# 384 bytes more in front of the left tiles of SBUF

## The chip, the cores and the metric

The kernel runs on one core of a Trainium2 chip. The metric is the device time of one execution in microseconds; the median of the runs counts. Names used below: PE is TensorE with its matmuls, PEld its weight loads, DVE is VectorE, ACT ScalarE, POOL GpSimd, SP SyncE (which issues most DMAs).

## What is computed

One layer of a decoder on 512 tokens of width 1024, in float32:

```python
h = h + 0.5 * swiglu(rmsnorm(h, ffn1_norm), ffn1_w_gate, ffn1_w_up, ffn1_w_down)   # 1024 -> 2816 -> 1024
proj = rmsnorm(h, mix_norm) @ w_in
u, v, z, xbc, dt_raw = split(proj)
ya = rmsnorm(chunked_spatial_gating(gelu(u), gelu(v), ...), gm_out_norm)
yb = mamba2_mixer(z, xbc, dt_raw, ...)
h = h + concatenate([ya, yb]) @ w_out
h = h + 0.5 * swiglu(rmsnorm(h, ffn2_norm), ffn2_w_gate, ffn2_w_up, ffn2_w_down)
h = h + sigmoid(rmsnorm(h, ple_norm) @ ple_w_gate + ple_b_gate) * (p @ ple_w_proj)
return rmsnorm(h, final_norm)
```

## The kernel before

The activations lie feature by feature: a tile is 128 features by 512 tokens, `h` is eight of them. Every large product is made of three matmuls in a rounded format (fp32r): an operand is split into a high part (`hi`, a copy rounded to fp32r) and a low part (`lo`, the rest), and `passes` (L468) issues hi by hi, hi by lo and lo by hi into one PSUM bank. For each unit of weights a DMA brings `raw` (128 by 1024), ACT makes `whi` from it and DVE `wlo` (`Unit.split` L438, `Parts.split` L682). A matmul has a stationary operand, 128 by 128 elements that a weight load brings into the array, and a moving operand that is streamed past it. In the profile's names `b<-x,whi` the moving operand stands first: `x` streams past `whi`.

The stages, in order of time:

- FFN 1 and FFN 2 (`swiglu`, L1028): the gate and up products of the groups 1 to 10 are done with seven products instead of eight for a 2-by-2 split (`Group.steps`, L869). The moving operands are the sums and differences of the input's halves, 256 tokens wide, in tiles `xfa` and `xfb` (`XForms`, L704); the stationary ones are `whi` and `wlo`. The products of group 0 (`plain_steps`, L930) take the same tiles with 512 tokens, in two runs of 256. The down products take `ghi` and `glo` as moving operands and `whix`, `wlox` (or `whi`, `wlo`) as weights.
- The mixer: `projection` (L1199), `first_step` and `dt_step` take the sixteen tiles `x` as moving operands, 512 wide, and `whi`, `wlo` as weights. `v_step` (L1544) turns this round: `whi` and `wlo` move, 512 wide, and 128-column slices of `x` are the weights. Then `out_step` (L1762) takes `ya` and `yb` as moving operands, with `whi`, `wlo`.
- The last stage (L1833 and on, here called PLE): eight units, `x` moving, 512 wide for the first five and in halves of 256 for the last three.

All operations are recorded and then issued in a fixed order, a list of some 2,500 units (`ORDER`, L87), by `issue` (L1935, the instruction itself at L1943, which is why every row of the profile says L1943).

SBUF of a partition is laid out so. A base pool `sb` holds what lives all the time: constants, `tmp`, `h`, `raw`, `whi`, `wlo` and small tiles. Above it stands a left region, and from the top end a right region is filled downwards. Each is opened anew as the stages go (`open_region` L336, `open_now` L342): left for FFN 1, for the mixer, for FFN 2 and for PLE, right for FFN 1, the mixer, FFN 2 and PLE. A new region's tiles may lie where tiles of the old one lay, and then wait for just those tiles (`reuse_waits="tile"`). Ahead of the tiles of a left region `open_now` puts a tile that nobody uses, `pad` (L331), of as many bytes per partition as `PAD` (L61) says:

```python
    def pad(pool, name):
        n = PAD[name.replace("1", "").replace("2", "")]
        if n:
            pool.tile([P, n // 4], F32, tag="pad", name=name_of("pad"))
```

From the order and the sizes of the tiles follows where each set begins in a partition. The base pool ends at byte 90,976. With the `PAD` of before:

| tiles | region | first byte | bytes each | remainder by 512 |
|---|---|---|---|---|
| `whi`, `wlo` (3 each) | base | 54,144 and 66,432 | 4,096 | 384 |
| `h`, `tmp`, `raw` | base | 25,472, 19,328, 41,856 | 2,048, 2,048, 4,096 | 384 |
| `xfa` (2), `xfb` (2) | left, FFN | 91,072 and 107,456 | 8,192 and 20,480 | 448 |
| `x` (16) | left, mixer and PLE | 91,136 | 2,048 | 0 |
| `xs` (8), `u` (9); `emb` (8) | left, mixer; PLE | 123,904 and 140,288; 123,904 | 2,048 | 0 |
| `ghi`, `glo`, `whix`, `wlox` | right, FFN | from 159,712 on | 4,096 | 480 |
| `ya`, `yb` (16 each) | right, mixer | 163,712 and 196,480 | 2,048 | 384 |

Within a tile, each weight load begins at a multiple of 512 bytes, and the moving operand of each fp32r matmul at a multiple of 1,024 (of 512 where `whi` and `wlo` move), so the remainder holds for all operands of a set. Copies of `raw0`, `F` and `embt` stand at the end of the FFN's left region.

Of the kernel before, what the change touches and what calls it, by code (L numbers as in the profile page):

```python
# [57 lines left out]

PAD = {"sb": 0, "ffn_left": 96, "mix_left": 160, "ple_left": 160, "ffn_right": 0, "mix_right": 96, "ple_right": 0}  # L61
HEADS = 16
HD = 64
GROUPS = 2
# [218 lines left out]
def layer_kernel(ctx: ExitStack, tc: tile.TileContext, a: dict, out: bass.AP):  # L283
# [47 lines left out]
# [4 lines that stand above are left out]
# [1717 lines left out]
```

## Time and profile before

| | us |
|---|---|
| three runs | 1115.97, 1113.59, 1114.28 |
| median of the runs | 1114.28 |
| the profiled execution | 1115.11 |
| its span, first to last instruction | 1113.4 |
| mean granted TensorE clock in it | 0.993 |

A row of instructions has the line, the engine and the operation, out<-in by the names of the tiles, the shape, the count, and then the busy time in us and the mean ns of one. The recorded duration of a matmul is longer than the distance from its start to the next one's start, since matmuls overlap in the array. What a matmul costs in a stream is that distance, and it is read from the timeline: the start of one row, the start of a later one, and the number of matmuls between. In a row of the timeline the first column is the start, the second the length of the merged row, and x2 says that it holds two matmuls. In a row of windows stand the stretch, its length, then the busy time and the count of each engine, the granted clock, the share of the DMA engines and GB/s.

### The profile page before, as it was taken

How to read it: one execution, taken by the hardware profiler on the slowest of the kernel's cores; microseconds unless marked ns; L12 is line 12 of the kernel's file. 1: busy time of each engine (PE TensorE's matmuls, PEld its weight loads, DVE VectorE, ACT ScalarE, POOL GpSimd, SP SyncE). 2: the span in 40 equal slices, each digit the busy share in tenths (PEclk: the TensorE clock that was granted, in tenths of full speed). 3: DMA queues.
4: the chain of work that ended last, by engine and by line, in shares of the span. 5: the costliest groups of instructions: out<-in, count | busy, mean ns of one | idle time of the engine just before them, and what ended most of it. 6: DMA issues, size and time to landing. Idle time of an engine off the chain costs nothing.

```text
span 1113.4 us, 16384 instructions
## 1 busy us (share of the span) xinstructions
PE 1099.0 (99%) x6631; PEld 967.6 (87%) x6631; DVE 765.0 (69%) x1072; ACT 520.2 (47%) x715; POOL 127.5 (11%) x124
## 2 busy tenths in 40 slices
PE   8999999999999999999999999999999999999996
PEld 6899999999998777778877878899999999999886
DVE  6977666666667468766649876687765666766656
ACT  7544443434435336866424444455434433434445
POOL 1100010000000200123103000101100000000212
PEclk9999999999999999999999999999999999999997
DMA  9788468564631224542314133767837674643412
GB/s 318 207 213 245 109 202 229 146 190 133 152 95 57 82 90 153 160 136 79 114 62 133 38 106 122 208 184 179 217 93 204 169 204 139 166 103 123 133 38 76
DMA packets 49036, 161.66 MB, mean 145 GB/s; under 512 B 5568, under 2 KB 5824, under 8 KB 48960
## 3 DMA queue, kind: packets, MB, share of 16 engines
q1 hardware_dynamic: 34128, 117.46, 31.3%
q0 software_dynamic: 9232, 33.56, 16.3%
q10 hardware_dynamic: 5600, 9.60, 2.9%
q8 instruction: 52, 0.85, 0.3%
q14 instruction: 24, 0.20, 0.1%
HBM read 156.33 MB, written 4.26 MB: 144 GB/s over the span
## 4 chain that ended last, share of the span: by engine, by line
PE 92%; DVE 5%; DMA 1%; ACT 1%; issue 1%; POOL 0%; ACTq 0%; SPq 0%; POOLq 0%
PE b L1943 92%; DVE tmp L1943 1%; DVE wlo L1943 1%; DVE xs L1943 1%; DMA g<-in_p 1%; DVE u L1943 0%; DVE x L1943 0%; DVE h L1943 0%; POOL ssum L1943 0%; DVE ya L1943 0%; DMA cs_dram<-csrow 0%; DVE yb L1943 0%; ACT tmp L1943 0%; DVE convin L1943 0%; ACT whi L1943 0%
## 5 line engine op out<-in xcount | busy, mean ns | idle before, releaser
L1943 PE MATMUL b<-xfb,whi 128*128 128x256 f32 (+1 forms) x1664 | 305.8, 284 | 0.0
L1943 PEld LDWEIGHTS b<-xfb,whi 128*128 128x128 f32 x1664 | 259.2, 188 | 7.0 <-issue 1.0
L1943 PE MATMUL b<-xfb,wlo 128*128 128x256 f32 (+1 forms) x832 | 236.3, 284 | 0.0
L1943 DVE TENSOR_TENSOR wlo<-raw,whi 128x1024 fp32r<-128x1024 f32 (+1 forms) x139 | 173.8, 1254 | 66.3 <-ACT whi L1943 66.3
L1943 ACT CAST whi<-raw 128x1024 fp32r<-128x1024 f32 (+1 forms) x140 | 145.1, 1040 | 147.5 <-PE b L1943 107.4
L1943 PE MATMUL b<-x,whi 128*128 128x512 f32 (+1 forms) x640 | 189.3, 382 | 0.7 <-ACT x L1943 0.4
L1943 PEld LDWEIGHTS b<-xfb,wlo 128*128 128x128 f32 x832 | 156.2, 188 | 1.4
L1943 PEld LDWEIGHTS b<-x,whi 128*128 128x128 f32 x640 | 116.1, 188 | 26.5 <-issue 1.5
L1943 PE MATMUL b<-xfa,whi 128*128 128x256 f32 (+1 forms) x704 | 134.4, 289 | 0.0
L1943 PE MATMUL b<-x,wlo 128*128 128x512 f32 (+1 forms) x312 | 117.9, 378 | 0.3 <-DVE wlo L1943 0.3
L1943 PE MATMUL b<-ghi,whix 128*128 128x512 f32 x296 | 116.6, 394 | 0.0
L1943 PE MATMUL b<-ghi,wlox 128*128 128x512 f32 x296 | 116.5, 394 | 0.0
L1943 PE MATMUL b<-glo,whix 128*128 128x512 f32 x296 | 115.3, 390 | 0.0
L1943 PEld LDWEIGHTS b<-xfa,whi 128*128 128x128 f32 x704 | 110.8, 188 | 3.9
L1943 PE MATMUL b<-xfa,wlo 128*128 128x256 f32 (+1 forms) x352 | 102.0, 290 | 0.0
L1943 ACT CAST whi<-rawb 128x1024 fp32r<-128x1024 f32 x52 | 54.5, 1048 | 79.7 <-PE b L1943 56.0
L1943 DVE TENSOR_TENSOR wlo<-rawb,whi 128x1024 fp32r<-128x1024 f32 x52 | 63.3, 1221 | 40.8 <-ACT whi L1943 40.7
L1943 DVE SCALAR_TENSOR_TENSOR h<-b,h 128x512 f32<-128x512 f32 x96 | 64.3, 685 | 29.3 <-PE b L1943 28.9
L1943 ACT CAST whix<-rawd 128x1024 fp32r<-128x1024 f32 (+1 forms) x40 | 39.4, 986 | 84.1 <-PE b L1943 73.2
L1943 PEld LDWEIGHTS b<-x,wlo 128*128 128x128 f32 x312 | 58.7, 188 | 12.6 <-DVE wlo L1943 1.0
L1943 PEld LDWEIGHTS b<-xfa,wlo 128*128 128x128 f32 x352 | 66.1, 188 | 1.4
L1943 DVE TENSOR_TENSOR wlox<-rawd,whix 128x1024 fp32r<-128x1024 f32 (+1 forms) x40 | 45.6, 1140 | 31.1 <-ACT whix L1943 31.1
(229 smaller groups left out, 1644.0 us busy)
## 6 DMA issues: line engine op xcount, KB each, us to landing
raw<-in_ffn_gu SPq DMA_DIRECT2D x56, 512.0 KB, 5.6
rawd<-in_ffn_down SPq DMA_DIRECT2D x40, 512.0 KB, 4.5
rawb<-in_ffn_gu SPq DMA_DIRECT2D x32, 512.0 KB, 5.7
raw<-in_ffn_gu POOLq DMA_DIRECT2D x30, 512.0 KB, 7.6
raw<-in_w_in SPq DMA_DIRECT2D x29, 512.0 KB, 3.7
s<-in_ffn_gu SPq DMA_DIRECT2D x20, 512.0 KB, 5.5
s<-in_ffn_gu POOLq DMA_DIRECT2D x20, 512.0 KB, 7.7
raw<-in_w_out SPq DMA_DIRECT2D x16, 512.0 KB, 3.7
```

The lines of the kernel that those rows point to most:

```text
L1943: getattr(getattr(real, engine), what)(*(real_of(x) for x in args), **{k: real_of(x) for k, x in kw.items()})
```

## The change

The three left layouts get 384 bytes more of the unused tile in front. Nothing else is changed: the same instructions in the same order.

```diff
-PAD = {"sb": 0, "ffn_left": 96, "mix_left": 160, "ple_left": 160, "ffn_right": 0, "mix_right": 96, "ple_right": 0}
+PAD = {"sb": 0, "ffn_left": 480, "mix_left": 544, "ple_left": 544, "ffn_right": 0, "mix_right": 96, "ple_right": 0}
```

So `xfa` and `xfb` begin at 91,456 and 107,840 (remainder by 512: 320 in place of 448), `x` at 91,520 (384 in place of 0), `xs`, `u` and `emb` at remainder 384 in place of 0. The base pool and the right regions stay.

## The prediction

> **What bounds the kernel.** I read the busy times and the chain of waits on the page first, then the groups of PE instructions by form, then windows, then the timeline of PE.
>
> ```profile
> span 1113.4 us, 16384 instructions
> PE 1099.0 (99%) x6631; PEld 967.6 (87%) x6631; DVE 765.0 (69%) x1072; ACT 520.2 (47%) x715; POOL 127.5 (11%) x124
> PE 92%; DVE 5%; DMA 1%; ACT 1%; issue 1%; POOL 0%; ACTq 0%; SPq 0%; POOLq 0%
> ```
>
> PE is busy 99% of the span and carries 92% of the chain that ends last. So the time is, nearly, the sum of the distances between matmul starts, and a change that touches these distances reaches the end almost undiminished.
>
> ```profile
> L1943 PE MATMUL b<-xfb,whi 128*128 128x256 f32 x1600 | 285.9, 279 | 0.0
> L1943 PE MATMUL b<-xfb,wlo 128*128 128x256 f32 x800 | 223.8, 280 | 0.0
> L1943 PE MATMUL b<-x,whi 128*128 128x512 f32 x544 | 172.1, 399 | 0.7 <-ACT x L1943 0.4 <-DVE x L1943 0.3
> L1943 PE MATMUL b<-xfa,whi 128*128 128x256 f32 x640 | 114.5, 279 | 0.0
> L1943 PE MATMUL b<-x,wlo 128*128 128x512 f32 x264 | 104.4, 395 | 0.3 <-DVE wlo L1943 0.3
> L1943 PE MATMUL b<-xfa,wlo 128*128 128x256 f32 x320 | 89.5, 280 | 0.0
> L1943 PE MATMUL b<-whi,x 128*128 128x512 f32 x128 | 42.7, 401 | 0.0
> L1943 PE MATMUL b<-wlo,x 128*128 128x512 f32 x64 | 25.3, 396 | 0.7 <-DVE wlo L1943 0.7
> ```
>
> These are the matmuls that read a tile on the left side. With `x`, 512 wide: 544 + 264 + 128 + 64 = 1000. With `xfa`, `xfb`, 256 wide: 1600 + 800 + 640 + 320 = 3360. What one costs in a stream stands in the timeline of PE. Here are, in pairs, the first and the last row of undisturbed stretches; in all of them one row is a lo and the next holds two hi, so a step from one lo row to the next is three matmuls.
>
> ```profile
> 672.64 0.39 PE L1943 MATMUL b<-ya,wlo 128*128 128x512 f32 x1
> ...
> 691.00 0.39 PE L1943 MATMUL b<-ya,wlo 128*128 128x512 f32 x1
> ```
>
> ```profile
> 400.72 0.39 PE L1943 MATMUL b<-x,wlo 128*128 128x512 f32 x1
> ...
> 414.72 0.39 PE L1943 MATMUL b<-x,wlo 128*128 128x512 f32 x1
> 421.76 0.39 PE L1943 MATMUL b<-x,wlo 128*128 128x512 f32 x1
> ...
> 424.55 0.39 PE L1943 MATMUL b<-x,wlo 128*128 128x512 f32 x1
> ```
>
> The first pair spans 81 matmuls in 18.36 us: 226.7 ns each (`ya`, on the right side). The second spans 60 in 14.00: 233.3 ns; the third 12 in 2.79: 232.5. Same form, same weights `whi` and `wlo`, yet `x` is 6.2 ns dearer on average of its two paces (232.9). The clock is not the reason:
>
> ```profile
> 367.00:427.00 60.00, 59.86 (x266) 48.09 (x267) 34.70 (x74) 21.37 (x28) 5.98 (x4) 1.00 0.26 81
> 427.00:452.00 25.00, 24.03 (x114) 18.98 (x113) 21.91 (x36) 16.70 (x26) 2.39 (x2) 1.00 0.56 173
> 655.00:712.00 57.00, 57.00 (x250) 46.68 (x251) 38.09 (x52) 26.79 (x38) 0.00 (x0) 1.00 0.43 138
> ```
>
> It is 1.00 in the windows of `x` (first row) and of `ya` (last). What differs is where the tiles lie. By the table of the layout, `ya` and the weights have the same remainder by 512 (384); `x` has 0, a distance of 128. I read the rows so: while one matmul streams, the next one's weights are read, and the two reads of SBUF disturb each other by an amount that depends on their distance modulo 512. That is an inference from the pace at two distances.
>
> Now the 256-wide stream:
>
> ```profile
> 760.48 0.28 PE L1943 MATMUL b<-xfb,wlo 128*128 128x256 f32 x1
> ...
> 772.49 0.28 PE L1943 MATMUL b<-xfa,wlo 128*128 128x256 f32 x1
> ```
>
> ```profile
> 754.95 0.28 PE L1943 MATMUL b<-xfb,wlo 128*128 128x256 f32 x1
> ...
> 757.33 0.28 PE L1943 MATMUL b<-xfb,wlo 128*128 128x256 f32 x1
> ```
>
> ```profile
> 1077.58 0.28 PE L1943 MATMUL b<-x,wlo 128*128 128x256 f32 x1
> ...
> 1084.70 0.28 PE L1943 MATMUL b<-x,wlo 128*128 128x256 f32 x1
> ```
>
> The usual pace is 102 matmuls in 12.01 us, 117.7 ns (`xfa`, `xfb`: remainder 448, distance +64). One stretch of the same tiles goes at 21 in 2.38 us, 113.3 ns: half of 226.7, so the undisturbed pace exists for this form too, but the stream seldom falls into it. `x` in halves, at distance 128, takes 60 in 7.12 us, 118.7 ns.
>
> **The change part by part.** No instruction, DMA or wait is added, removed or moved past another. The three left layouts shift alike, so which tiles of successive left layouts share bytes stays as it was. The left side's highest byte goes from 158,720 to 159,104, still below the lowest of the right (159,552), so no tile of the right comes to wait for one of the left. What changes are the remainders.
>
> *x, 512 wide.* The remainder becomes 384, the weights' own, in both roles: `x` streaming past `whi`, and `whi` streaming past `x` (where `x` is the weights). That is the geometry of `ya` with `whi`, so I take its pace: 232.9 - 226.7 = 6.2 ns less on 1000 matmuls, 6.2 us. Three things come off. After an interruption the stream needs some matmuls until it reaches the good pace:
>
> ```profile
> 619.23 0.40 PE L1943 MATMUL b<-yb,wlo 128*128 128x512 f32 x1
> ...
> 621.30 0.39 PE L1943 MATMUL b<-yb,wlo 128*128 128x512 f32 x1
> ```
>
> These nine took 2.07 us, 230.0 ns each, 0.03 us too much. 1000 matmuls in units of 24 are some 42 stretches; interrupted at each, and at about 0.04 us, that is 1.5 us; uninterrupted it is 0. I take 0.9. Second, from 427 to 452 us the chain runs over DVE and a DMA, and the 114 matmuls there have slack: 114 x 6.2 ns = 0.7 us do not count. Third, DVE's and ACT's order behind a faster PE: DVE is busy 34.70 of 60 us in the first window, so it follows, and I take 0.2 us. Left: 6.2 - 0.9 - 0.7 - 0.2 = 4.4 us.
>
> *xfa and xfb, 256 wide.* The remainder goes from 448 to 320, the distance to the weights from +64 to -64. No row shows -64. The nearest are +64 (117.7 ns), 128 (118.7) and the rare good pace (113.3). From below it is bounded by 113.3: 3360 x 4.4 ns = 14.8 us gained. From above I use the 512-wide rows: the undisturbed 226.7 goes up to 233.3, one step of 6.67 ns per matmul; the same step on 113.3 gives 120.0, 2.3 ns over today: 7.7 us lost. I take no change, since -64 is as far from the weights as +64 and 117.7 lies between both ends. This is the largest unknown by far.
>
> *The rest.* The 192 matmuls of group 0 (512 wide, two runs of 256 from `xfa`, `xfb`) share that unknown: 226.7 to 233.3 around
>
> ```profile
> 719.04 0.39 PE L1943 MATMUL b<-xfb,wlo 128*128 128x512 f32 x1
> ...
> 723.16 0.39 PE L1943 MATMUL b<-xfb,wlo 128*128 128x512 f32 x1
> ```
>
> 18 in 4.12 us, 228.9 ns: -0.4 to +0.8 us, taken as 0. The 144 half matmuls of `x` in PLE could fall from 118.7 to 113.3 (0.8 us), but the chain there is on DVE and ACT: taken as 0. DVE and ACT do not mind the remainder:
>
> ```profile
> L1943 DVE TENSOR_TENSOR u<-u,tmp 128x512 f32<-128x512 f32 x8 | 5.3, 686 | 0.0
> L1943 DVE TENSOR_TENSOR ssum<-ssum,tmp 128x512 f32<-128x512 f32 x21 | 14.5, 689 | 12.9 <-ACT tmp L1943 11.3 <-ACT ssum L1943 1.3
> ```
>
> `u` at remainder 0 with `tmp` at 384 takes 686 ns, both at 384 take 689: 0. The DMAs into the moved tiles (`raw0`, `u`, `xs`, `emb`) are few and PE's chain has 1% of DMA: 0, and at worst a fraction of that 1%.
>
> [...]
>
> **Sum.** On the profiled execution: 1115.1 - 4.4 = 1110.7. It lies 0.8 above the median of the runs (1114.28), so for the median I predict 1109.9.
>
> **Rivals.** (a) *The FFN stream falls into the good pace.* For: the 21 matmuls at 113.3 ns show that this pace needs no other tiles. Against: it was reached once, at +64, and nothing says that -64 is better. Price: up to 14.8 us more, 1095.1; half of it, 1102.5. (b) *-64 is worse than +64.* Each weight load meets the stream once more, 6.67 ns on the undisturbed pace, 120.0 ns: it costs 7.7 + 0.8 us and gives 1118.4, slower than before. It decides from the point where the 3360 matmuls lose over 4.4 us, 1.3 ns each (119.0 ns). For: no distance that the rows show but 0 is free, and 128 is worse than 64. Against: 118.7 at 128 is the worst pace of this form that I see. (c) *Distance is not the cause*, but something else that `x` and `ya` do not share, such as what DVE or the DMAs do beside them; then nothing happens: 1114.3. Against: `ya` holds its pace for 81 matmuls with DMA at 0.43, `x` its dearer one with DMA at 0.26.
>
> **How the numbers follow.** Differences within 0.2% (2.2 us) a measurement of this kernel cannot tell from no change. Forecast 0.42 (0.36 faster, 0.06 same, where the interruptions eat more); (a) 0.20, all faster; (b) 0.24, of which 0.16 slower and 0.08 where its loss just cancels the gain; (c) 0.14, of which 0.10 same and 0.02 on either side. Faster 0.58, same 0.24, slower 0.18. The range goes from 1100.0 (two thirds of (a)) to 1117.5 (nearly all of (b)); both signs are in it, and the forecast's own range, with the interruptions at either end and 0.3 ns on the FFN stream, is 1108 to 1112.
>
> **What would show it.** In the timeline of the changed kernel: `x` past `whi` and `whi` past `x` at 226.7 ns once past an interruption (right), or still at 232 to 233 (the inference falls, (c)). The `xfb` stream at 117.7 (forecast), 113.3 (a) or 119 to 120 (b); one look at it decides the sign. `ya`, `ghi` with `whix`, DVE and ACT durations unchanged; if they move, the layout does more than I think.

## The result, and the profile after

| | before | changed |
|---|---|---|
| median of four runs, us | 1113.93 (1112.53 to 1115.97) | 1096.41 (1095.51 to 1097.21) |
| span of the profiled execution, us | 1113.4 | 1094.7 |
| ratio | | 0.9841, 95% interval 0.9824 to 0.9858 |

The changed kernel is 17.5 us faster. (Among the executions of the experiments, three took 1344.74, 1799.88 and 2690.17 us; they are in no time or ratio given here.) The prediction was 1109.9, with a range down to 1100.0, so the time lies below it, near rival (a) with its 1095.1. The top of the page of the changed kernel (span, busy time of each engine, the chain):

```profile
span 1094.7 us, 16384 instructions
PE 1079.9 (99%) x6631; PEld 951.9 (87%) x6631; DVE 764.9 (70%) x1072; ACT 520.4 (48%) x715; POOL 127.0 (12%) x124
PE 91%; DVE 4%; DMA 1%; ACT 1%; POOL 1%; issue 1%; ACTq 0%; SPq 0%; POOLq 0%; DVEq 0%
```

The counts are those of before, PE is still busy 99% of the span, and DVE, ACT and POOL have the busy times of before within 0.5 us. PE alone lost 19.1 us of busy time (1099.0 to 1079.9). So the same matmuls follow each other more closely.

The timeline of PE in the changed kernel shows where. As in the prediction, each fence holds the first and the last row of an undisturbed stretch, with one lo row per three matmuls. First the 256-wide stream in FFN 1, 25 such rows:

```profile
71.11 0.28 PE L1943 MATMUL b<-xfb,wlo 128*128 128x256 f32 x1
...
79.27 0.28 PE L1943 MATMUL b<-xfa,wlo 128*128 128x256 f32 x1
```

72 matmuls in 8.16 us: 113.3 ns. This is the good pace that the kernel before reached in one rare stretch; here nearly the whole stream holds it, 3,217 of 3,357 matmuls. Next, `x` in the mixer (11 rows), and group 0, 512 wide (7 rows):

```profile
535.99 0.39 PE L1943 MATMUL b<-x,wlo 128*128 128x512 f32 x1
...
542.79 0.39 PE L1943 MATMUL b<-x,wlo 128*128 128x512 f32 x1
```

```profile
25.23 0.39 PE L1943 MATMUL b<-xfa,wlo 128*128 128x512 f32 x1
...
29.43 0.39 PE L1943 MATMUL b<-xfa,wlo 128*128 128x512 f32 x1
```

`x` takes 30 matmuls in 6.80 us, 226.7 ns, the pace of `ya`. Group 0 takes 18 in 4.20 us, 233.3 ns: it has become dearer. Last, the halves of `x` in the last stage (27 rows):

```profile
1060.64 0.28 PE L1943 MATMUL b<-x,wlo 128*128 128x256 f32 x1
...
1070.00 0.28 PE L1943 MATMUL b<-x,wlo 128*128 128x256 f32 x1
```

78 in 9.36 us, 120.0 ns, dearer than the 118.7 of before.

Summed over both traces: the table takes the distance from each matmul's start to the next start, by stream, without those over 250 ns (512 wide) or 135 ns (256 wide), which I count as waits.

| stream | matmuls | before, ns | changed, ns | difference, us |
|---|---|---|---|---|
| `xfa`, `xfb`, 256 wide | 3357, 3356 | 117.63 | 113.67 | -13.4 |
| `x` past `whi`, `wlo`, 512 wide | 783, 781 | 232.76 | 227.46 | -4.6 |
| `whi`, `wlo` past `x` | 180 | 232.67 | 227.82 | -0.9 |
| `ghi`, `glo` past `whix`, `wlox` | 888 | 230.40 | 229.81 | -0.5 |
| group 0 | 191 | 229.28 | 233.16 | +0.7 |
| halves of `x` | 144 | 118.69 | 119.94 | +0.2 |

Together -18.5 us, of the 18.7 that the span lost. (Each row counts its own number of matmuls; `x` has two fewer after, which is 0.5 us of its 4.6.) `ya` and `yb` stay at 227.5 ns, `ghi` past `whi` and `wlo` at 233.3. All of the span that lies outside these undisturbed streams is 94.8 us before and 94.6 after: no wait came or went.

### The profile page after: what moved, and what is told of

It reads as the page before. It is cut to its first block, busy times and chain, and to the rows that moved or that the text cites. A ratio compares the mean times of both kernels' runs of the same rounds, so it can differ in the third digit from the quotient of the medians.

```text
span 1094.7 us, 16384 instructions
## 1 busy us (share of the span) xinstructions
PE 1079.9 (99%) x6631; PEld 951.9 (87%) x6631; DVE 764.9 (70%) x1072; ACT 520.4 (48%) x715; POOL 127.0 (12%) x124
## 4 chain that ended last, share of the span: by engine, by line
PE 91%; DVE 4%; DMA 1%; ACT 1%; POOL 1%; issue 1%; ACTq 0%; SPq 0%; POOLq 0%; DVEq 0%
PE b L1943 91%; DVE tmp L1943 1%; POOL ssum L1943 1%; DVE xs L1943 1%; DMA g<-in_p 1%; DMA u<-cs_dram 0%; DVE u L1943 0%; DVE x L1943 0%; DVE wlo L1943 0%; DVE h L1943 0%; DMA cs_dram<-csrow 0%; ACT tmp L1943 0%; ACT L1943 0%; DVE yb L1943 0%; ACT whi L1943 0%
## 5 line engine op out<-in xcount | busy, mean ns | idle before, releaser
L1943 PE MATMUL b<-xfb,whi 128*128 128x256 f32 (+1 forms) x1664 | 296.6, 281 | 0.0
L1943 PEld LDWEIGHTS b<-xfb,whi 128*128 128x128 f32 x1664 | 256.3, 188 | 7.4 <-issue 1.0
L1943 PE MATMUL b<-xfb,wlo 128*128 128x256 f32 (+1 forms) x832 | 234.1, 281 | 0.0
L1943 PE MATMUL b<-x,whi 128*128 128x512 f32 (+1 forms) x640 | 186.8, 378 | 0.7 <-ACT x L1943 0.5
L1943 PE MATMUL b<-xfa,whi 128*128 128x256 f32 (+1 forms) x704 | 130.7, 287 | 0.0
L1943 PE MATMUL b<-x,wlo 128*128 128x512 f32 (+1 forms) x312 | 116.7, 374 | 0.6 <-DVE wlo L1943 0.6
```

The lines of the kernel that those rows point to most:

```text
L1943: getattr(getattr(real, engine), what)(*(real_of(x) for x in args), **{k: real_of(x) for k, x in kw.items()})
```

## The experiments

All kernels differ from the kernel before in the `PAD` line alone, where nothing else is said. A distance is the address of the moving operand minus that of the weights, modulo 256. The mean paces come from the trace of each run in the way of the table above.

### Each part alone

```diff
+PAD = {"sb": 0, "ffn_left": 480, "mix_left": 160, "ple_left": 160, "ffn_right": 0, "mix_right": 96, "ple_right": 0}
```

> Only the FFN's left pad gets the 384 bytes; the pads of the mixer and of PLE stay at 160, so x is at distance 128 from its weights as before. Theory (the pace of a stream goes by the distance from the moving operand to the weights, modulo 512): the 256-wide xfa and xfb stream goes at 113.5 ns instead of 117.7, 13.3 us less on 3360 matmuls; the 192 of group 0 go up to 233 ns (+0.6 us); x stays at 232 to 233 ns. Time 1113.9 - 13.3 + 0.6 - 0.5 (ghi, glo as in the changed kernel) = 1100.7, at most 1102. Rival (the gain of the changed kernel hangs on the shift of all three layouts, or on the order of work in the mixer): about as before, 1110 or more.

Measured: 1100.46 us (median of four), ratio 0.9884 (0.9867 to 0.9900). `xfa` and `xfb` at 113.67 ns, group 0 at 233.16, `x` at 232.69.

```diff
+PAD = {"sb": 0, "ffn_left": 96, "mix_left": 544, "ple_left": 544, "ffn_right": 0, "mix_right": 96, "ple_right": 0}
```

> Only the pads of the mixer and of PLE get the 384 bytes; the FFN's stays at 96, so xfa and xfb are at distance +64 as before. Theory (distance): x past whi and wlo, and whi and wlo past x, go at 227.5 ns instead of 232.7; the halves of x in PLE at 120.0 instead of 118.7 (+0.2 us); xfa and xfb stay at 117.7. In the trace of the changed kernel the x streams gave 3.5 us and the short operations between them some 1 to 2 us: time 1113.9 - 4.5 = 1109.4, from 1108 to 1111. Rival (x gives nothing by itself): 1113.9, or x at 232 ns.

Measured: 1110.12 us, ratio 0.9967 (0.9957 to 0.9978). `x` at 227.45 ns, `xfa` and `xfb` at 117.63. The product of the two ratios is 0.9851, within the interval of the whole change: the two parts add up, and three quarters come from the FFN's pad.

### What the distance is measured to

The weights move instead of the activations: 128 bytes in front of the whole base pool (`e3_base`), or in front of `whi` alone (`e5_weights`), with the left pads set so that `xfa`, `xfb` and `x` keep their remainders of before.

```diff
+PAD = {"sb": 128, "ffn_left": 480, "mix_left": 32, "ple_left": 32, "ffn_right": 384, "mix_right": 480, "ple_right": 0}
...
+    pad(base, "sb")
     homes["base"].open(base)
```

> The weights are moved instead of the activations: 128 bytes in front of the base pool, so whi, wlo, h, tmp and raw have remainder 0 in place of 384; the left pads are set so that xfa, xfb and x keep the remainders of before (448 and 0), and the right pads so that ya, yb and ghi keep their distance from whi. So the distances are those of the changed kernel (-64 and 0) and the remainders of the moving tiles those of before. Theory (the distance decides): as the changed kernel, 1096.4, within 1.5 us: xfa, xfb at 113.5 ns, x at 227.5, halves of x at 120.0. Rival (the place of the moving tile itself decides, whatever the weights): as before, 1113.9, with 117.7 and 232.7 ns.

Measured: 1098.29 us, ratio 0.9857 (0.9840 to 0.9874). In the timeline of this kernel (27 rows; the line is 1944 as one was added):

```profile
72.93 0.28 PE L1944 MATMUL b<-xfb,wlo 128*128 128x256 f32 x1
...
81.77 0.28 PE L1944 MATMUL b<-xfa,wlo 128*128 128x256 f32 x1
```

78 matmuls in 8.84 us: 113.3 ns, with `xfa` and `xfb` at the remainder of before. The place of the moving tile by itself is not what counts.

```diff
+PAD = {"sb": 128, "ffn_left": 480, "mix_left": 32, "ple_left": 32, "ffn_right": 384, "mix_right": 480, "ple_right": 0}
...
             for tag, (shape, dt) in self.tags.items():
+                if tag == "whi":
+                    pad(pool, "sb")
                 n = 8 if self.pool is psum else BUFS.get(tag, 1)
```

> As the run with the base pool moved, but the 128 bytes stand right in front of whi, so that h, tmp and raw keep their places and only whi, wlo and the small tiles behind them move; xfa, xfb and x have the remainders of before, and distances of -64 and 0 from the weights. Theory (the weights are the other end of the distance): 1097, within 1.5 us, xfa and xfb at 113.7 ns, x at 227.5. Rival (the other end is what DVE, ACT and the DMAs do in h, tmp and raw): as before, 1114, xfa and xfb at 117.6 ns.

Measured: 1099.13 us, ratio 0.9866 (0.9853 to 0.9880), a little above the bound of 1098.5 that the theory gave; its span was 1096.4 us, `xfa` and `xfb` at 113.95 ns, `x` at 227.35. With `h`, `tmp` and `raw` in their old places the paces are still near those of the changed kernel (113.67 and 227.46): the weights (and not `h`, `tmp` or `raw`) are the other end of the distance.

```diff
+PAD = {"sb": 0, "ffn_left": 224, "mix_left": 288, "ple_left": 288, "ffn_right": 0, "mix_right": 96, "ple_right": 0}
```

> All left pads 256 bytes less than in the changed kernel (224, 288, 288): xfa and xfb at distance +192 from the weights, x at 256. Theory with a period of 256 bytes: as the changed kernel, 1096.4 within 1.5 us, xfa and xfb at 113.5 ns, x at 227.5. Theory with a period of 512: other paces, xfa and xfb anywhere from 113.3 to 120 ns and x above 229 ns, so a time over 1098. Rival (the place of the moving tile decides): other paces as well.

Measured: 1097.28 us, ratio 0.9849 (0.9831 to 0.9868), 113.67 and 227.45 ns: at the two distances tried, 256 bytes less make no difference.

### The other distances

Five kernels with the three left pads at other values; the FFN's pad sets the distance of `xfa` and `xfb`, the other two that of `x`.

```diff
+PAD = {"sb": 0, "ffn_left": 32, "mix_left": 96, "ple_left": 96, "ffn_right": 0, "mix_right": 96, "ple_right": 0}
```

> Left pads 32, 96, 96: xfa and xfb at distance 0 from the weights (modulo 256), x at +64. Theory (each width has its own best distance): 256 wide at distance 0 goes at 120.0 ns, as the halves of x in PLE did in the changed kernel; group 0 at 226.7; x at +64 at 229 ns, as group 0 did before. Against before 3360 x 2.3 = 7.7 us more, 192 x 2.5 = 0.5 less, 1000 x 3.7 = 3.7 less: 1114 + 3.5 = 1117.5. Rival (distance 0 is the best for every width): xfa and xfb at 113.3 ns, 1114 - 14.8 - 4.2 = 1095.

> Left pads 160, 224, 224: xfa and xfb at distance 128, x at -64 (modulo 256). Theory (each width has its own best distance): xfa and xfb at 118.7 ns, as the halves of x at 128 before; x at 233.2 ns, as group 0 at -64 in the changed kernel. Against before 3360 x 1.1 = 3.7 us more, 1000 x 0.5 = 0.5 more, 192 x 4 = 0.8 more: 1119. Rival (-64 is good for every width): x at 227 ns, 1114 + 3.7 + 0.8 - 5.5 = 1113.

> Left pads 0, 64, 64: xfa and xfb at distance -32, x at +32. No run has shown these. If the pace changes evenly between the distances known, xfa and xfb lie between 113.5 (at -64) and 120.0 (at 0), 116.8 ns, and x between 227.5 (at 0) and 229 (at +64), 228.3: 1114 - 2.8 - 4.4 = 1107. Rival (the good distance is a narrow one): xfa and xfb at 119 to 120 ns, 1114 + 6 - 4.4 = 1116.

> Left pads 64, 0, 0: xfa and xfb at distance +32, x at -32. If the pace changes evenly between the distances known, xfa and xfb lie between 120.0 (at 0) and 117.7 (at +64), 118.9 ns, and x between 227.5 (at 0) and 233.2 (at -64), 230.4: 1114 + 4.2 - 2.3 = 1116. Rival (+32 belongs to the good side of the 256-wide stream): xfa and xfb near 113.5, 1114 - 13.8 - 2.3 = 1098.

> Left pads 192, 128, 128: xfa and xfb at distance -96 (160 modulo 256), x at +96. At the odd multiples of 32 measured so far (+32 and -32) 512 wide went at 233.2 and 233.1 ns and 256 wide at 116.7 and 118.2. Theory (only multiples of 64 have a good pace): xfa and xfb between 116 and 119, x at 233.3, as ghi past whi at +96 did: 1114 + 0 (from -5 to +4) + 0.6 + 0.8 = 1115. Rival (even change between the distances known): xfa and xfb between 118.7 (at 128) and 113.7 (at -64), 116.2, x between 229.2 and 232.7, 231: 1114 - 4.8 - 1.7 = 1107.

| run | time, us | ratio |
|---|---|---|
| `s1_0_64` | 1118.92 | 1.0044 (1.0027 to 1.0061) |
| `s2_128_m64` | 1116.73 | 1.0022 (1.0009 to 1.0035) |
| `s3_m32_32` | 1117.21 | 1.0038 (1.0022 to 1.0054) |
| `s4_32_m32` | 1111.53 | 0.9986 (0.9974 to 0.9997) |
| `s5_m96_96` | 1119.46 | 1.0045 (1.0030 to 1.0060) |

By the time alone, `s1` came out by its theory and `s3` by its rival, `s2` and `s4` lie between the two, and `s5` lies above both, nearer to its theory. The mean pace of each stream by distance, from all runs, in ns; where a field has several figures, they are from different runs, and the reason follows below:

| distance | `xfa`, `xfb`, 256 wide | halves of `x` | `x`, 512 wide | group 0, 512 wide |
|---|---|---|---|---|
| 0 | 119.8 | 119.9 | 227.5 | 227.6 |
| 32 | 116.7 | 116.7 | 233.2 | 233.3 |
| 64 | 117.3 to 117.8 | 113.4, 117.8 | 229.2 | 229.3 |
| 96 | | 120.0 | 233.4 | |
| 128 | 118.7 | 118.7 | 232.8 | 233.2 |
| 160 | 118.5 | | | 234.1 |
| 192 (-64) | 113.7, 113.9, 117.5 | 113.4 | 233.3 | 233.2 |
| 224 (-32) | 118.2 | 118.4 | 233.2 | 233.2 |

Two streams of one width and distance agree within 0.9 ns, but for 256 wide at 64 and -64. The widths differ: 0 is the best distance for 512 wide and nearly the worst for 256 wide; at -64, 256 wide has its best pace (in most runs) and 512 wide a dear one. So the expectation that took each width for itself held in `s1` and for the paces of `s2`. The even change between known distances that I had supposed in `s3` and `s4` fell: `x` at 32 went at 233.2 in place of 228.3, `xfa` and `xfb` at -32 at 118.2 in place of 116.8. Of the distances tried, none is the best for both widths.

### The attempt at a better kernel, and what it showed

```diff
+PAD = {"sb": 0, "ffn_left": 480, "mix_left": 544, "ple_left": 96, "ffn_right": 96, "mix_right": 96, "ple_right": 0}
```

> The changed kernel with two more pads: PLE's left pad 96 instead of 544, so x in PLE is at distance +64, where its halves went at 113.4 ns instead of 119.9 (144 x 6.5 = 0.9 us) and its whole tiles at 229.2 instead of 227.5 (some 100 x 1.7 = 0.2 us back); and the FFN's right pad 96 instead of 0, so ghi and glo are at distance 0 from whi and wlo instead of 96: 216 x (233.3 - 227.5) = 1.2 us. Theory: 1096.4 - 0.9 + 0.2 - 1.2 = 1094.5, 0.9823 of before. Rival (both are hidden behind DVE or given back in the streams' starts): 1096.4.

Measured: 1105.90 us, ratio 0.9933 (0.9920 to 0.9947), 9.5 us slower than the changed kernel. Both gains came: the halves of `x` at 113.36 ns, `ghi` and `glo` past `whi` and `wlo` at 226.92 in place of 233.36, and past `whix` at 226.68 in place of 229.81. But `xfa` and `xfb`, which were not moved, went back to 117.47 ns.

So something besides the distance sets the pace. The changed kernel shows it too, on a small scale. These are two neighbouring stretches in its FFN 1, of the same two tile sets at the same distance; between them stand two matmuls of `tmp` and a short pause:

```profile
48.23 0.28 PE L1943 MATMUL b<-xfb,wlo 128*128 128x256 f32 x1
...
50.71 0.28 PE L1943 MATMUL b<-xfb,wlo 128*128 128x256 f32 x1
...
51.93 0.28 PE L1943 MATMUL b<-xfb,wlo 128*128 128x256 f32 x1
...
62.47 0.28 PE L1943 MATMUL b<-xfa,wlo 128*128 128x256 f32 x1
```

The first takes 21 matmuls in 2.48 us (118.1 ns), the second 93 in 10.54 (113.3). By the whole trace, five stretches of the changed kernel with 140 matmuls together go at 117.8 ns and all others at 113.3; the same five do so in `e1_ffn`, `e4_m256` and `b2_ple` (the last kernel below), so it isn't chance. In the kernel before it is the reverse: one stretch of 24 at 113.3, all others at 117.8. In none of these traces does a stretch change its pace before something interrupts it, and the longest has 120 matmuls. So each pace lasts through an undisturbed stretch, and the means above say how many stretches were in which.

Theory H says that a 256-wide stream at +64 or at -64 has two paces which hold themselves, and that what runs before picks one. Four more kernels ask for it. Two leave `xfa` and `xfb` at +64 and move only `ghi` (the FFN's right pad at 160, as here, and at 96):

```diff
+PAD = {"sb": 0, "ffn_left": 96, "mix_left": 160, "ple_left": 160, "ffn_right": 160, "mix_right": 96, "ple_right": 0}
```

> The kernel before with only the FFN's right pad at 96, so ghi and glo are at distance 0 from whi and wlo; xfa and xfb stay at +64, where they went at 117.6 ns. Theory H (two paces hold themselves at +64 and at -64, and the stream before picks one): the change of ghi's place can flip xfa and xfb to 113.4 ns: 1114 - 14.2 - 3 (ghi at 226.7) - 2.4 (its weights' side) = 1095 to 1097. Theory D (the distance alone decides): xfa and xfb at 117.6 ns, 1114 - 3.3 - 2.4 = 1108 to 1111.

Measured: 1111.97 us, ratio 0.9981 (0.9971 to 0.9992), a little above what theory D allowed; `xfa` and `xfb` at 117.77 ns. Two stretches of 24 alone went at 113.3 ns: this run hardly tells H from D.

> The kernel before with only the FFN's right pad at 160, so ghi and glo are at distance -64 from whi and wlo; xfa and xfb stay at +64. Theory H: may flip to 113.4 ns, 1114 - 14 = 1100, or hold 117.6, 1114; it can't say which from the runs so far. Theory D: 117.6 ns, 1114.

Measured: 1111.89 us, ratio 0.9975 (0.9964 to 0.9986), mean 117.29 ns. Behind the mean stand both paces. In the timeline of this kernel, three stretches of `xfa` and `xfb` (8, 40 and 8 lo rows), with `ghi` past `whix` between them:

```profile
68.77 0.28 PE L1943 MATMUL b<-xfb,wlo 128*128 128x256 f32 x1
...
71.24 0.28 PE L1943 MATMUL b<-xfb,wlo 128*128 128x256 f32 x1
...
72.98 0.28 PE L1943 MATMUL b<-xfb,wlo 128*128 128x256 f32 x1
...
86.25 0.28 PE L1943 MATMUL b<-xfb,wlo 128*128 128x256 f32 x1
...
87.95 0.28 PE L1943 MATMUL b<-xfa,wlo 128*128 128x256 f32 x1
...
90.43 0.28 PE L1943 MATMUL b<-xfa,wlo 128*128 128x256 f32 x1
```

21 matmuls in 2.47 us (117.6 ns), then 117 in 13.27 (113.4), then 21 in 2.48 (118.1): same form, same tiles, same distance, and the pace changes only where six matmuls of `ghi` and `glo` stand between.

The third leaves `xfa` and `xfb` at -64, as changed, and puts `ghi` at another distance at which it has the same pace:

```diff
+PAD = {"sb": 0, "ffn_left": 480, "mix_left": 544, "ple_left": 544, "ffn_right": 160, "mix_right": 96, "ple_right": 0}
```

> The changed kernel with only the FFN's right pad at 160, so ghi and glo are at distance -64 from whi and wlo, where 512-wide streams went at 233.2 ns as they did at 96; xfa and xfb stay at -64. Theory D: xfa and xfb at 113.7 ns, 1096.4. Theory H: 113.7 and 1096.4, or 117.5 and 1109.

Measured: 1108.33 us, ratio 0.9945 (0.9927 to 0.9963), `xfa` and `xfb` at 117.47 ns. Its timeline shows the moment of the flip: 28 lo rows, then the first `ghi` past `whix` and past `whi`, then, from 66.29 us on, `xfb` again; the last pair spans 27 lo rows.

```profile
52.81 0.28 PE L1943 MATMUL b<-xfb,wlo 128*128 128x256 f32 x1
...
61.99 0.28 PE L1943 MATMUL b<-xfa,wlo 128*128 128x256 f32 x1
...
63.49 0.40 PE L1943 MATMUL b<-ghi,whi 128*128 128x512 f32 x1
...
66.06 0.39 PE L1943 MATMUL b<-ghi,wlo 128*128 128x512 f32 x1
66.29 0.40 PE L1943 MATMUL b<-xfb,whi 128*128 128x256 f32 x2
...
70.74 0.28 PE L1943 MATMUL b<-xfb,wlo 128*128 128x256 f32 x1
...
79.92 0.28 PE L1943 MATMUL b<-xfa,wlo 128*128 128x256 f32 x1
```

Up to the first `ghi` 81 matmuls take 9.18 us (113.3 ns, as in the changed kernel); after it the same 9.18 us hold only 78 (117.7 ns), and so it stays to the end of FFN 1. (In FFN 2 one stretch of 119 goes at 113.3 ns again.) The changed kernel at the same place goes on at 113.3 (the first fence of its timeline). `ghi` past `whi` itself goes at the same mean pace in both: here 11 matmuls from 63.49 to 66.06, 233.6 ns, and in the changed kernel 11 from 63.97 to 66.54:

```profile
63.97 0.39 PE L1943 MATMUL b<-ghi,whi 128*128 128x512 f32 x1
...
66.54 0.39 PE L1943 MATMUL b<-ghi,wlo 128*128 128x512 f32 x1
```

So it isn't the mean speed of the stream before that decides (233.6 ns in both, then 117.7 ns here and 113.3 there), but something that goes with the place of its tiles. The single steps do differ: by the starts in the trace, three come in turn as 232, 237 and 231 ns in the changed kernel, and two as 236 and 231 here.

The last kernel is the attempt without its FFN part:

```diff
+PAD = {"sb": 0, "ffn_left": 480, "mix_left": 544, "ple_left": 96, "ffn_right": 0, "mix_right": 96, "ple_right": 0}
```

> The changed kernel with only PLE's left pad at 96 instead of 544; the FFN as in the changed kernel. Theory H (the slow run was slow because of ghi's place): xfa and xfb at 113.7 ns, halves of x at 113.4: 1096.4 - 0.9 + 0.2 = 1095.7. Rival (the slow run was slow because of PLE's pad, or by chance): xfa and xfb at 117.5 ns, 1108.

Measured: 1097.31 us, ratio 0.9853 (0.9840 to 0.9867), `xfa` and `xfb` back at 113.67 ns: PLE's pad had no part in the slow run, `ghi`'s place had. But the halves of `x` went at 117.81 ns here and at 113.36 in `b1_best`, with all tiles of PLE at the same addresses in both. In the timeline of `b2_ple` (27 rows) and of `b1_best` (30 rows):

```profile
1059.65 0.28 PE L1943 MATMUL b<-x,wlo 128*128 128x256 f32 x1
...
1068.84 0.28 PE L1943 MATMUL b<-x,wlo 128*128 128x256 f32 x1
```

```profile
1068.31 0.28 PE L1943 MATMUL b<-x,wlo 128*128 128x256 f32 x1
...
1078.17 0.28 PE L1943 MATMUL b<-x,wlo 128*128 128x256 f32 x1
```

78 matmuls in 9.19 us (117.8 ns) against 87 in 9.86 (113.3). That is theory H at +64, with nothing changed in the stage itself. Theory D, the distance alone, falls. In both kernels 512-wide matmuls of `x` run straight into the halves, in a rhythm of about 226, 229 and 232 ns; but the last step ahead of the halves is the one of 232 in `b1_best` and the one of 229 in `b2_ple`. So the same rhythm arrives one step apart. That is a lead, and no kernel was made to test it. No kernel tried beats the changed one: `b2_ple` is the same within its interval.

## Why the prediction was wrong, and where it was right

**What bounds the kernel** held: PE's chain took the whole gain, 18.5 us in the streams and 18.7 in the span, and no wait took its place.

**That distance is the cause**, which the prediction inferred from two tiles, held for `x`: moving the weights does the same as moving the activations (`e3_base`, `e5_weights`). The modulus was too large, 256 instead of 512 (`e4_m256`: 113.67 and 227.45 ns with 256 bytes less). For the 256-wide stream the distance is half of the cause: at +64 and at -64 it leaves two paces open, 113.3 and 117.8 ns. That it works through two reads of SBUF that disturb each other was an inference of mine, and so was the weight load that "meets the stream once more" in rival (b): no run shows it. The runs show paces by distance: in `e5_weights`, 128 bytes more in front of `whi`, with the moving tiles at their old remainders, brought the 256-wide stream from 117.63 to 113.95 ns and the time down by 1.3% (the gain of `x` included).

**`x`, 512 wide**, was right in its cause, the distance, and in size. The two streams gained 5.3 and 4.9 ns per matmul, where 6.2, less 0.9 for the starts, was expected: together about 5.0 us on 961 undisturbed matmuls (781 x 5.30 + 180 x 4.85). With the part alone the ratio was 0.9967, some 3.7 us, against 4.4 us net. That the 0.9 came out so well was in part luck: it was picked from between 0 and 1.5, and 42 starts at 0.04 us are 1.7.

**The 256-wide stream is the step that failed**: "I take no change, since -64 is as far from the weights as +64 and 117.7 lies between both ends." It took the size of the distance for what sets the pace, and put the largest term of the sum at nothing by that argument. Measured: 117.63 to 113.67 ns, 13.4 us of gain, near the bound of 14.8 that the same paragraph had worked out. What the runs put in its place: at +64 and at -64 alike the stream has two paces, 113.3 and 117.8 ns, and an undisturbed stretch is wholly in one of them. Today's 117.7 was therefore no value between two ends but one of the two. With `ghi` where it is in this kernel, nearly every stretch at -64 starts in the good pace and nearly every one at +64 in the bad one. With `ghi` at two other places (`f3_m64_r160`, `b1_best`) the stream at -64 had a mean of 117.47 ns, so that "no change" would have been nearly right for this stream. Distance -64 allows the gain; that this kernel got it was not to be read from the rows of before, and why it did stays open.

The rare stretch pointed to the two paces: it held 113.3 ns from its first row quoted to its last, and the stretches around it 117.7, with the same tiles at the same addresses. The rows said that both exist; which of them the stream takes at -64 they didn't say.

**Rival (a)** was the case that came, with 13.4 of its 14.8 us; it had been given 0.20. The range cut it off: its end at 1100.0 stood for two thirds of (a), but nearly all stretches can go over together, so the range had to reach 1095. **Rival (b)** came in no run at -64: the dear pace there is 117.8 ns. Its 120.0, and so its 1118.4, is what the stream shows at distance 0 (`s1_0_64`: 119.78 ns, 1118.92). **Rival (c)** fell.

**The rest.** Group 0 lost 0.7 us, at the upper bound of 0.8. The halves of `x`, taken as 0 with a chance of a gain, lost 0.2. `ghi` past `whix`, which was to stay, gained 0.5 us with its distance unchanged: here the layout did more than the prediction thought (230.40 to 229.81 ns). Whether that goes with the stream before, or with the distance from `xfa` and `xfb` to `whix` at each change from one stream to the other, which went from -32 to 96, no run shows. DVE, ACT and the DMAs showed nothing, as expected: `u` from `u` and `tmp` on DVE took 686 ns before and 685 after, `x` from `h` on ACT 716 and 717, and the DMAs into `u` and `emb` landed after 4.0 and 3.3 us before and 4.1 and 3.4 after (medians).

**What stays open.** Which property of the stream before picks the pace. In `f2_64_r160` the good one followed six matmuls of `ghi` at 232.5 ns and the bad one six at 226.3; but in `f3_m64_r160` and the changed kernel the stream before had one mean pace and the outcomes differed. The distances at the change of streams can't be all of it, since in PLE they are the same in `b1_best` and `b2_ple`; the step at which a rhythm arrives is untested. A model that would foretell the pace from addresses wasn't found, and why the distance changes the pace no run tells.

## What to carry to other kernels

When one form of matmul shows several paces in a timeline at full clock, compare the addresses of the moving operand and of the weights (here modulo 256, by `e4_m256`: 113.67 and 227.45 ns with 256 bytes less); a pad of some hundred bytes was worth up to 5 per cent of such a stream here (119.8 to 113.7 ns), and its best value isn't the same for 256 and 512 columns (113.7 ns at -64, 227.5 at 0). Here a stream had two paces at one address (113.3 and 117.8 ns), and which one it took changed when only tiles that it doesn't read were moved, so move one region at a time, and look again at every stream in the trace, also at those that weren't moved. Where the trace shows a cost in two states, forecast the states, with a chance for each: staying in today's state is one of them, and not a safe middle.

## What was not expected of the hardware

- A distance of 0 is the best for 512 columns (227.5 ns) and nearly the worst for 256 (119.8 ns); at -64 it is 233.2 and, in the changed kernel, 113.7.
- Two paces at the same addresses: 113.36 and 117.81 ns in the last stage of `b1_best` and `b2_ple`, 113.67 and 117.47 ns in the FFN of the changed kernel and of `f3_m64_r160`, where only tiles that this stream doesn't read were moved (`ghi`, `glo`, `whix`, `wlox`), by 160 bytes. That alone is worth 11.9 us (1096.41 against 1108.33).
